# Low halves of weight pieces computed on GpSimd during two kinds of stage, in a two-sequence hybrid encoder

## The chip, the cores and the metric

The kernel runs on 1 core of one Trainium2 chip, as one launch. The metric is device time in microseconds, and lower is better. The engines are named as the profile names them: PE is TensorE (PEld its weight loads), DVE is VectorE, ACT is ScalarE, POOL is GpSimd, SP issues the DMAs. Each engine works through its own instructions in order and waits on semaphores for the others.

## What is computed

Two sequences, a prompt of 512 tokens and a sample of 256, go through the same two layers. Each layer is a SwiGLU, a mixer of three head groups side by side (RG-LRU, RWKV-7 in both directions, attention), and a second SwiGLU:

```python
def layer(x, c, lp, rope):
    mod = (jax.nn.silu(c) @ lp["w_ada"] + lp["b_ada"])[:, None, :]
    sh1, sc1, g1, sh2, sc2, g2, sh3, sc3, g3 = jnp.split(mod, N_MOD, axis=-1)
    h = rmsnorm(x, lp["norm_g"][0]) * (1 + sc1) + sh1
    x = x + 0.5 * g1 * swiglu(h, lp["ffn_w_in"][0], lp["ffn_w_out"][0])
    h = rmsnorm(x, lp["norm_g"][1]) * (1 + sc2) + sh2
    x = x + g2 * mixer(h, lp, rope)          # concat(LRU, RWKV, attention) @ w_mix_out
    h = rmsnorm(x, lp["norm_g"][2]) * (1 + sc3) + sh3
    x = x + 0.5 * g3 * swiglu(h, lp["ffn_w_in"][1], lp["ffn_w_out"][1])
    return x

def step(st, inp):                           # RWKV: 64x64 state of a head, one token
    r_t, w_t, k_t, v_t, kk_t, b_t = inp
    sa = jnp.einsum("bhvk,bhk->bhv", st, -kk_t)
    st = st * w_t[:, :, None, :] + sa[..., None] * b_t[:, :, None, :] + v_t[..., None] * k_t[:, :, None, :]
    y = jnp.einsum("bhvk,bhk->bhv", st, r_t)
    return st, y
```

Width is 1024, the feed-forward width 2816, and all is in fp32.

## The kernel before

**Dense products.** Activations lie transposed (channels on the partitions, tokens along the row), so a product is a sum over tiles of 128 x 128 weights. For accuracy each fp32 operand is split into a high half in the matmul's own format and a low half, and three products stand for one: high x high, high x low, low x high (`mm3`). Weights are streamed from memory in raw tiles `wr` of up to 1024 columns (4 buffers, `weight_raw`, SP) and taken apart piece by piece, 512 or 128 columns each, in `wload`: ACT copies the raw piece into the high half `wh` (L269), then DVE subtracts that from the raw piece to give the low half `wl` (L270). There are 7 buffers of `wh` and 7 of `wl`, shared by both sequences; a buffer comes free when PE has read it for the last time. There are 1368 pieces, 684 for each sequence. One piece is used by 12 matmuls if it has 512 columns of weights (4 tiles x 3 products) and by 3 if it has 128.

**Two sequences against each other.** `layer_thread` runs once for the prompt (`PS`) and once for the sample (`SS_`). While one sequence is in its RWKV stage, which is a long chain of small matmuls with vector work between them, the dense products of the other fill PE. The order of PE's instructions is written out by `Sched`, a planner with threads, priorities and fixed waiting times (`LAT`): the program puts matmuls on PE in exactly that order and PE keeps to it, so a late operand stops PE there. The other engines' instructions are put in order by the framework's own scheduler.

**Fetching ahead.** `wfill` keeps a queue of converted pieces for each sequence: 4 ahead while the other sequence has its flag `mixing` set, otherwise 1 ahead (`LOOK`, `look`). The flag is set when a sequence has put out its mixer's input product (`mix_in`, 19 tiles `mip`) and cleared when it starts its output product (`wopen`). Between the two lie the end of attention and LRU and the RWKV stage, `rwkv_pair` for two pairs of heads in turn.

**A pair of heads.** `rwkv_pair` has, in this order: a preparation (norm of the keys through `kkp` and a reciprocal square root of some ten tiny DVE instructions, L355 to L362; then `AR` and `BK` at L780 to L792, with POOL's share at L747, L781 and L789); the score products `scps`; four levels of a blockwise triangular inverse (`yps`, `dps`); a chain over chunks of 64 tokens (`saps`, `stps`, `zps`, with POOL's `spt` at L970); and an end part, in which the result `ywp` is normalised (L996 to L1006, again with the tiny instructions of a reciprocal square root), transposed through `yp` and multiplied by the gate.

**Stages by the clock of the profile.** The prompt's `mix_in` runs from 486 to 701 us and again from 2025 to 2224; its RWKV stage from 701 to 1020 and from 2224 to 2547, beside the sample's feed-forward (`pb`, `ops`). The sample's `mix_in` runs from 1005 to 1187 and from 2780 to 2899; its RWKV stage from 1187 to 1466 and from 2899 to 3176, beside the prompt's feed-forward (`pg`, `pu`, `ops`).

Of the kernel before, what the change touches and what calls it, by code (L numbers as in the profile page):

```python
# [7 lines left out]
F32 = mybir.dt.float32  # L8
# [3 lines left out]
ALU = mybir.AluOpType  # L12
# [99 lines left out]
def trunk_kernel(ctx, tc, xT, cT, wadh, wada, wfi, wfo, wmi, wmo, prm, gatew, loraw, cst, rope, scanm, outT, dbg=None):  # L112
    nc = tc.nc
    V, A, G, PE = nc.vector, nc.scalar, nc.gpsimd, nc.tensor
# [79 lines left out]
    PS, SS_ = Seq(0), Seq(1)  # L194
# [69 lines left out]
    def wtile(dt, name):  # L264
        return wsp.tile([128, 512], dt, name=name, tag=name)

    def wload(raw, n):
        hi, lo = wtile(F32R, "wh"), wtile(F32R, "wl")
        A.activation(out=hi[:, :n], in_=raw, func=AF.Copy)  # L269
        V.tensor_tensor(out=lo[:, :n], in0=raw, in1=hi[:, :n].bitcast(F32), op=ALU.subtract)  # L270
        return hi, lo

    def weight_units():
        for l in range(DEPTH):
            for fi in range(2):
                if fi == 1:
                    for mt in range(19):
                        yield wmi[l, mt]
                    yield None
                    for m in range(8):  # L280
                        yield wmo[l, m]
                prev = None
                for f0, nf in GROUPS:
                    for p in range(f0, f0 + nf):
                        yield wfi[l, fi, 2 * p]
                        yield wfi[l, fi, 2 * p + 1]
                        if prev is not None:
                            for m in range(8):
                                yield wfo[l, fi, m, :, prev[0] * 128:(prev[0] + prev[1]) * 128]
                            prev = None  # L290
                    prev = (f0, nf)
                for m in range(8):
                    yield wfo[l, fi, m, :, prev[0] * 128:(prev[0] + prev[1]) * 128]

    def weight_raw(u):
        raw = wsp.tile([128, 1024], F32, name="wr", tag="wr", bufs=NR)
        nc.sync.dma_start(out=raw[:, :u.shape[-1]], in_=u)
        return raw

    def weight_list(q):  # L300
        us = weight_units()
        if q is PS:
            raws = [weight_raw(next(us)) for t in range(4)]
            for c in (0, 512):
                for raw in raws:
                    yield raw[:, c:c + 512], 512
        for u in us:
            if u is None:
                yield None
                continue  # L310
            n = u.shape[-1]
            raw = weight_raw(u)
            for c in range(0, n, 512):
                yield raw[:, c:min(c + 512, n)], min(512, n - c)

    def wfill(q, n):
        while len(q.wq) < n:
            if q.wnext is None:
                q.wnext = next(q.wl, False)
                if q.wnext is None:  # L320
                    q.wstop = True
            if q.wnext is False or q.wstop:
                break
            q.wq.append(wload(*q.wnext))
            q.wnext = None

    def wopen(q):
# [701 lines left out]
    def layer_thread(q, th):  # L1029
# [18 lines left out]
        for l in range(DEPTH):  # L1048
# [18 lines left out]
            M = Mix()  # L1067
            M.stage, M.orw, M.lru_done = 0, [], False
            tl = [sch.spawn(attention(q, l, M)), sch.spawn(lru(q, l, M))]
            yield from mix_in(q, l, xs, M)  # L1070
            q.mixing = True
            xs = None
            n2.x = None
            yield lambda: all(t.done for t in tl)
# [51 lines left out]
    with tc.manual_schedule(engines={mybir.EngineType.PE}):  # L1126
        head = Norm(PS, 0, 0)
        for m in range(KD):
            head.add(m, V)
        head.stats()  # L1130
        for q in (PS, SS_):
            q.wl, q.wq, q.wnext, q.wstop, q.mixing = weight_list(q), [], None, False, False
        mods_done.update(((0, 0), (0, 1)))
        first = [(dbank(name="pg"), dbank(name="pu")) for p in range(2)]
        fb = [b for f in first for b in f]
        app = head.apply()
        fw = []

        def head_mm(c):
            for k in (2 * c, 2 * c + 1):  # L1140
                if k % 4 == 0:
                    fw[:] = [wget(PS) for b in fb]
                xh, xl = head.x[k]
                z = (k % 4) * 128
                for b, (wh, wl) in zip(fb, fw):
                    for i, (wt, xt) in enumerate(((wh, xh), (wh, xl), (wl, xh))):
                        mm(b, wt[:, z:z + 128], xt, start=(k == 0 and i == 0), stop=(k == KD - 1 and i == 2))

        for c in range(4):
            ada_head(c)  # L1150
            next(app)
            next(app)
            if c == 0:
                wfill(PS, 4)
            if c > 0:
                head_mm(c - 1)
        head_mm(3)
        th = {}
        th[0] = sch.spawn(layer_thread(PS, th), dense=True, prio=1)
        th[1] = sch.spawn(layer_thread(SS_, th), dense=True, prio=-2)  # L1160
        sch.spawn(ada_rest(), prio=-1)
        sch.run()
# [111 lines left out]
```

## Time and profile before

| | us |
|---|---|
| median of 3 runs | 3485.95 (3485.34 to 3487.81) |
| the profiled execution, its own time | 3480.19 |
| its span, first to last instruction | 3478.4 |
| PE busy in the span | 3344.5 (96%) |
| DVE busy | 2011.8 (58%), 906.0 of it at L270 |
| ACT busy | 1441.6 (41%) |
| POOL busy | 525.2 (15%) |

The busy share of an engine is an average over stages with different limits, so the profile is to be read stage by stage. A busy PE can still be a PE that works through small matmuls at the pace of another engine; what tells is where it sits idle, at which granted clock it runs, and how long before its first use an operand was ready.

### The profile page before, as it was taken

The numbers are of one execution on the slowest core, as the hardware profiler recorded it, in microseconds if no ns is written. First come the engines' busy times: TensorE is split into PE (matmuls) and PEld (weight loads), VectorE is DVE, ScalarE is ACT, GpSimd is POOL, SyncE is SP. The second block draws the span as 40 slices with busy tenths as digits, with TensorE's granted clock in tenths as the row PEclk, the third lists the DMA queues.
The fourth block names the chain that finished last, engine by engine and source line by source line (L and its number), as shares of the span: only waits on it lengthen the run. The fifth ranks groups of instructions, "written<-read, shape, count | busy, mean of one in ns | idle before, by whom it ended". The sixth has DMA issues, their size and how long they took to land.

```text
span 3478.4 us, 69138 instructions
## 1 busy us (share of the span) xinstructions
PE 3344.5 (96%) x28052; PEld 2742.5 (79%) x28052; DVE 2011.8 (58%) x3973; ACT 1441.6 (41%) x2730; POOL 525.2 (15%) x659
## 2 busy tenths in 40 slices
PE   7999999989889999999999999989899999999999
PEld 6777776678877777888888876778789978778899
DVE  4433365776667645556333476657567676456466
ACT  3322244644345533334333337434345564334354
POOL 1100020222121211112000111212211112111010
PEclk9999999999989999999999999999899999999999
DMA  7666674133243222333333331233245533223455
GB/s 279 217 210 199 211 261 142 61 100 115 87 152 97 94 81 78 122 99 122 91 94 91 124 106 57 74 107 103 82 150 170 174 116 101 68 86 119 146 179 161
DMA packets 151629, 445.79 MB, mean 128 GB/s; under 512 B 16912, under 2 KB 20752, under 8 KB 151312
## 3 DMA queue, kind: packets, MB, share of 16 engines
q1 hardware_dynamic: 151312, 441.39, 39.7%
q8 instruction: 220, 3.60, 0.4%
q14 instruction: 97, 0.79, 0.1%
HBM read 427.17 MB, written 14.16 MB: 127 GB/s over the span
## 4 chain that ended last, share of the span: by engine, by line
PE 67%; DVE 7%; issue 3%; ACT 2%; POOL 1%; DMA 0%; POOLq 0%; DVEq 0%; ACTq 0%
PE ops L148 20%; PE pb L148 11%; PE pg L148 11%; PE pu L148 11%; PE mip L148 5%; DVE wl L270 2%; PE dps L148 1%; PE yps L148 1%; DVE nx L411 1%; PE S L148 1%; PE avp L148 1%; PE ywp L148 1%; DVE SC L829 1%; PE ptp L163 1%; ACT wh L269 1%
## 5 line engine op out<-in xcount | busy, mean ns | idle before, releaser
L269 ACT ACTIVATE wh<-wr 128x512 fp32r<-128x512 f32 (+1 forms) x1368 | 812.6, 600 | 1605.3 <-PE ops L148 518.6
L270 DVE TENSOR_TENSOR wl<-wr,wh 128x512 fp32r<-128x512 f32 (+1 forms) x1368 | 906.0, 668 | 783.4 <-ACT wh L269 750.7
L148 PE MATMUL ops<-an,wh 128*128 128x512 f32 (+1 forms) x2816 | 718.2, 346 | 15.5 <-POOL an L351 6.4
L148 PEld LDWEIGHTS ops<-an,wh 128*128 128x128 f32 x2816 | 483.8, 191 | 90.2 <-issue 10.1
L148 PE MATMUL pb<-xn,wh 128*128 128x256 f32 x2816 | 526.9, 288 | 1.0 <-issue 1.0
L148 PE MATMUL ops<-an,wl 128*128 128x512 f32 (+1 forms) x1408 | 479.4, 340 | 5.6 <-DVE wl L270 5.5
L148 PEld LDWEIGHTS pb<-xn,wh 128*128 128x128 f32 x2816 | 438.5, 191 | 18.0 <-issue 10.5
L148 PE MATMUL pg<-xn,wh 128*128 128x512 f32 x1408 | 449.2, 400 | 0.0
L351 POOL TENSOR_TENSOR an<-sg,an 128x512 fp32r<-128x512 f32 (+1 forms) x176 | 201.7, 1146 | 1632.8 <-ACT an L350 1524.3
L148 PE MATMUL pu<-xn,wh 128*128 128x512 f32 x1408 | 448.1, 399 | 0.0
L148 PE MATMUL pb<-xn,wl 128*128 128x256 f32 x1408 | 399.8, 284 | 18.9 <-DVE wl L270 17.0
L430 DVE SCALAR_TENSOR_TENSOR x<-ops,gat,x 128x512 f32<-128x512 f32 (+1 forms) x352 | 215.9, 614 | 215.9 <-PE ops L148 210.7
L148 PE MATMUL mip<-xn,wh 128*128 128x512 f32 (+1 forms) x1216 | 317.4, 351 | 4.2 <-DVE xn L417 1.9
L148 PEld LDWEIGHTS pg<-xn,wh 128*128 128x128 f32 x1408 | 260.5, 189 | 66.1 <-issue 4.3
L148 PEld LDWEIGHTS pu<-xn,wh 128*128 128x128 f32 x1408 | 259.7, 188 | 66.1 <-issue 7.6
L148 PEld LDWEIGHTS ops<-an,wl 128*128 128x128 f32 x1408 | 269.6, 191 | 39.3 <-DVE wl L270 6.1
L148 PEld LDWEIGHTS pb<-xn,wl 128*128 128x128 f32 x1408 | 269.0, 191 | 23.0 <-DVE wl L270 20.1
L148 PE MATMUL pg<-xn,wl 128*128 128x512 f32 x704 | 277.6, 394 | 2.2 <-DVE wl L270 2.2
L148 PE MATMUL pu<-xn,wl 128*128 128x512 f32 x704 | 276.7, 393 | 0.0
L148 PEld LDWEIGHTS mip<-xn,wh 128*128 128x128 f32 x1216 | 211.2, 194 | 45.1 <-issue 11.6
L148 PE MATMUL mip<-xn,wl 128*128 128x512 f32 (+1 forms) x608 | 208.5, 343 | 2.2 <-DVE wl L270 2.2
L148 PEld LDWEIGHTS pg<-xn,wl 128*128 128x128 f32 x704 | 133.0, 189 | 33.7 <-DVE wl L270 2.6
(256 smaller groups left out, 3727.2 us busy)
## 6 DMA issues: line engine op xcount, KB each, us to landing
wr<-in_wfi_dram SPq DMA_DIRECT2D x352, 512.0 KB, 3.6
adaw<-in_wada_dram SPq DMA_DIRECT2D x128, 512.0 KB, 4.4
wr<-in_wfo_dram SPq DMA_DIRECT2D x192, 256.0 KB, 2.7
wr<-in_wfo_dram SPq DMA_DIRECT2D x128, 320.0 KB, 2.9
wr<-in_wmi_dram SPq DMA_DIRECT2D x76, 512.0 KB, 3.6
wr<-in_wmo_dram SPq DMA_DIRECT2D x32, 512.0 KB, 3.5
adaw<-in_wadh_dram SPq DMA_DIRECT2D x32, 256.0 KB, 5.2
xsp<-x SPq DMA_DIRECT2D x8, 512.0 KB, 3.0
```

The costliest lines, as they stand in the source:

```text
L148: PE.matmul(out, lhsT, rhs, start=start, stop=stop, skip_group_check=True)
L163: PE.transpose(out, src, idn)
L269: A.activation(out=hi[:, :n], in_=raw, func=AF.Copy)
L270: V.tensor_tensor(out=lo[:, :n], in0=raw, in1=hi[:, :n].bitcast(F32), op=ALU.subtract)
L351: eng.tensor_tensor(out=lo, in0=src, in1=hi.bitcast(F32), op=ALU.subtract)
L411: V.scalar_tensor_tensor(out=t, in0=q.x[k], scalar=scl[l][:, i, k, q.i:q.i + 1], in1=self.rB, op0=ALU.mult, op1=ALU.mult)
L430: V.scalar_tensor_tensor(out=q.x[m], in0=ps, scalar=gat[l][:, i, m, q.i:q.i + 1], in1=q.x[m], op0=ALU.mult, op1=ALU.add)
L829: V.tensor_tensor(out=SC[h][d][:, c0:c0 + 4, :], in0=pp[h].rearrange("p (c x) -> p c x", x=128), in1=smask[d].unsqueeze(1).to_broadcast([1 ...
```

## The change

The low half is computed by POOL instead of DVE in two cases: while the other sequence has `mixing` set, and while the piece's own sequence is in `mix_in` (new flag `inmix`). In all other cases DVE goes on computing it. The instruction is the same one, a subtraction of two operands in SBUF. Nothing else is edited; PE's instructions and their order stay the same to the last row.

```diff
-    def wload(raw, n):
+    def wload(q, raw, n):
         hi, lo = wtile(F32R, "wh"), wtile(F32R, "wl")
         A.activation(out=hi[:, :n], in_=raw, func=AF.Copy)
-        V.tensor_tensor(out=lo[:, :n], in0=raw, in1=hi[:, :n].bitcast(F32), op=ALU.subtract)
+        eng = G if (SS_ if q is PS else PS).mixing or q.inmix else V
+        eng.tensor_tensor(out=lo[:, :n], in0=raw, in1=hi[:, :n].bitcast(F32), op=ALU.subtract)
         return hi, lo
...
-            q.wq.append(wload(*q.wnext))
+            q.wq.append(wload(q, *q.wnext))
...
+            q.inmix = True
             yield from mix_in(q, l, xs, M)
-            q.mixing = True
+            q.mixing, q.inmix = True, False
```

In the built program 567 of the 1368 low halves stand on POOL, 511 of 512 columns and 56 of 128; POOL has 1226 instructions where it had 659. (Line numbers behind `wload` are higher by one in the changed kernel: L270 becomes L271, L781 becomes L782.)

The first place is the preparation of the prompt's first pair (703 to 736 us in the profile). On POOL, from `csum` to `aa` (`AR` and `aa` are the preparation's own steps, `an` belongs to the sample's feed-forward), there stood before:

```order
L747 TENSOR_SCALAR csum<-csum 128x1024
L753 MEMSET Pt 128x8
L754 MEMSET Pt 128x8
L768 COPY PC<-Pt 128x8
L781 TENSOR_TENSOR AR<-f,Pt 128x512
L769 COPY PC<-Pt 128x8
L351 TENSOR_TENSOR an<-sg,an 128x256
L781 TENSOR_TENSOR AR<-f,Pt 128x512
L789 TENSOR_TENSOR aa<-aa,f 128x1024
```

and now, from the second `AR` on:

```order
L782 TENSOR_TENSOR AR<-f,Pt 128x512
L271 TENSOR_TENSOR wl<-wr,wh 128x512 x6
L790 TENSOR_TENSOR aa<-aa,f 128x1024
L271 TENSOR_TENSOR wl<-wr,wh 128x512 x6
L352 TENSOR_TENSOR an<-sg,an 128x256
```

Six low halves stand between the preparation's last two steps on POOL, and more between the earlier ones. On DVE, in the same place, from the normalised keys on (`x` is the sample's residual), there stood before:

```order
L762 TENSOR_TENSOR kb<-kb,rB 128x512
L430 SCALAR_TENSOR_TENSOR x_112<-ops,gat_134,x_112 128x256
L780 SCALAR_TENSOR_TENSOR AR<-kb,Pt 128x512 x2
L783 SCALAR_TENSOR_TENSOR csum<-aa,kb 128x1024
L270 TENSOR_TENSOR wl<-wr,wh 128x512
L786 SCALAR_TENSOR_TENSOR BK<-csum,cu 128x8x64 x2
L430 SCALAR_TENSOR_TENSOR x_113<-ops,gat_134,x_113 128x256
L270 TENSOR_TENSOR wl<-wr,wh 128x512
L788 TENSOR_SCALAR aa<-aa,kah_3965,ka_0_3963 128x1024
L270 TENSOR_TENSOR wl<-wr,wh 128x512
```

and now:

```order
L763 TENSOR_TENSOR kb<-kb,rB 128x512
L431 SCALAR_TENSOR_TENSOR x_112<-ops,gat_134,x_112 128x256
L781 SCALAR_TENSOR_TENSOR AR<-kb,Pt 128x512 x2
L784 SCALAR_TENSOR_TENSOR csum<-aa,kb 128x1024
L431 SCALAR_TENSOR_TENSOR x_112<-ops,gat_134,x_112 128x256
L787 SCALAR_TENSOR_TENSOR BK<-csum,cu 128x8x64 x2
L431 SCALAR_TENSOR_TENSOR x_113<-ops,gat_134,x_113 128x256
L789 TENSOR_SCALAR aa<-aa,kah_3965,ka_0_3963 128x1024
```

The low halves are gone from between the preparation's steps on DVE; the steps themselves keep their order. The second place is the end part of the same pair (837 to 848 us); on POOL there stood before, between the chain over chunks and the next pair:

```order
L970 TENSOR_SCALAR spt<-S_7809,PC 128x64 x12
L351 TENSOR_TENSOR an<-sg,an 128x256 x3
L1014 TENSOR_TENSOR yy<-yy,kb 128x512
L351 TENSOR_TENSOR an<-sg,an 128x256
L747 TENSOR_SCALAR csum<-csum 128x1024
```

and now, from the last `spt` on:

```order
L971 TENSOR_SCALAR spt<-S_7809,PC 128x64 x2
L271 TENSOR_TENSOR wl<-wr,wh 128x512 x2
L352 TENSOR_TENSOR an<-sg,an 128x256
L271 TENSOR_TENSOR wl<-wr,wh 128x512 x5
L352 TENSOR_TENSOR an<-sg,an 128x256
L271 TENSOR_TENSOR wl<-wr,wh 128x512 x3
L352 TENSOR_TENSOR an<-sg,an 128x256
L271 TENSOR_TENSOR wl<-wr,wh 128x512 x2
L1015 TENSOR_TENSOR yy<-yy,kb 128x512
```

Twelve low halves now stand on POOL ahead of the step `yy` of the end part.

## Rows read from the trace of the kernel before

**Rows 1.** Busy time by stage: length, busy us of each engine, clock, DMA share, GB/s.

```profile
core 0: us, PE busy (x) PEld busy (x) DVE busy (x) ACT busy (x) POOL busy (x), PEclk, DMA share, GB/s
701.00:1020.00 319.00, 284.99 (x4744) 253.85 (x4743) 215.13 (x448) 132.65 (x262) 67.76 (x86) 0.94 0.36 115
...
1187.00:1466.00 279.00, 278.63 (x2662) 217.30 (x2662) 149.16 (x326) 96.17 (x193) 41.74 (x59) 1.00 0.29 88
...
2224.00:2547.00 323.00, 287.11 (x4777) 258.84 (x4776) 211.52 (x441) 134.00 (x263) 74.18 (x89) 0.92 0.34 105
```

**Rows 2.** The same view for the prompt's four preparations and one end part.

```profile
703.00:736.00 33.00, 28.52 (x209) 25.18 (x208) 28.55 (x57) 17.42 (x34) 10.17 (x9) 1.00 0.40 124
853.00:886.00 33.00, 30.27 (x226) 27.58 (x226) 29.01 (x53) 16.72 (x29) 10.96 (x10) 0.96 0.35 108
2226.00:2260.00 34.00, 30.37 (x217) 27.23 (x217) 25.97 (x51) 15.74 (x32) 13.99 (x12) 0.95 0.26 75
2379.00:2412.00 33.00, 29.00 (x204) 26.78 (x201) 26.84 (x50) 15.66 (x27) 11.09 (x10) 0.90 0.38 118
835.00:850.00 15.00, 14.29 (x167) 13.78 (x164) 12.97 (x32) 7.53 (x15) 1.52 (x2) 1.00 0.37 106
```

**Rows 3.** Busy time of the low halves alone on DVE: length, busy us, count.

```profile
703.00:736.00 33.00, 12.96 (x19) 1.00 0.40 124
716.29:733.62 17.33, 7.34 (x11) 1.00 0.59 182
837.18:847.78 10.60, 4.10 (x6) 1.00 0.40 116
```

**Rows 4.** Groups by shape: line, engine, operation, count, busy us, mean ns, idle before.

```profile
L270 DVE TENSOR_TENSOR wl<-wr,wh 128x512 fp32r<-128x512 f32 x1240 | 867.3, 705 | 705.2 <-ACT wh L269 676.4 <-PE ops L148 10.0 <-PE pu L148 5.9
...
L351 POOL TENSOR_TENSOR an<-sg,an 128x512 fp32r<-128x512 f32 x88 | 116.9, 1329 | 1056.9 <-ACT an L350 1056.9
...
L270 DVE TENSOR_TENSOR wl<-wr,wh 128x128 fp32r<-128x128 f32 x128 | 40.6, 317 | 78.2 <-ACT wh L269 74.3 <-PE ops L148 2.0 <-PE saps L148 1.7
```

**Rows 5.** Timeline of PE in the first preparation and end part: start, us, idle before.

```profile
710.83 1.02 PE L148 MATMUL kkp<-ksq,cs 128*128 128x512 f32 x2
...
727.43 0.39 PE L148 MATMUL pb<-xn,wl 128*128 128x256 f32 x1 [2.26 <-DVE wl L270]
...
736.22 0.37 PE L148 MATMUL scps<-AR,BK 64*128 64x128 f32 x1
...
848.62 1.15 PE L148 MATMUL yp<-cs,yy 64*64 64x64 f32 x32 [0.70 <-DVE yy L1006]
```

**Rows 6.** Timeline of DVE in the first preparation.

```profile
716.29 0.70 DVE L367 STREAM_TRANSPOSE tT<-kkp 128x512 f32<-128x512 f32 x1
...
731.21 2.48 DVE L270 TENSOR_TENSOR wl<-wr,wh 128x512 fp32r<-128x512 f32 x1
733.62 1.28 DVE L792 TENSOR_TENSOR BK<-aa,cu 128x512 f32<-128x512 f32 x2
```

**Rows 7.** Timeline of POOL, end of the first preparation and end part.

```profile
730.37 2.77 POOL L789 TENSOR_TENSOR aa<-aa,f 128x1024 f32<-128x1024 f32 x1 [14.75 <-DVE aa L788]
...
842.34 0.76 POOL L351 TENSOR_TENSOR an<-sg,an 128x256 fp32r<-128x256 f32 x1 [12.67 <-PE pb L148]
```

**Rows 8.** Timeline of DVE in the end part of the first pair.

```profile
837.18 0.69 DVE L996 TENSOR_REDUCE st<-ywp 128x8 f32<-128x512 f32 x1 [1.54 <-PE ywp L148]
...
842.40 0.72 DVE L360 TENSOR_TENSOR nt<-y 128x8 f32<-128x8 f32 x1
...
844.58 0.17 DVE L360 TENSOR_TENSOR nt<-y 128x8 f32<-128x8 f32 x1
...
847.78 0.69 DVE L1006 TENSOR_TENSOR yy<-yy,rs 128x512 f32<-128x512 f32 x1
```

**Rows 9.** Waits of PE between 2224 and 2547 us: total us, times, longest.

```profile
PE zps L148 <- DVE S L971: 4.6, 5, 2.5
```

**Rows 10.** Timeline of DVE in the end part of the second pair.

```profile
995.40 0.72 DVE L355 TENSOR_SCALAR sh<-va 128x8 int32<-128x8 int32 x1
```

More of the change, by code (lines that the diff above doesn't have):

```diff
@@ L1131, in trunk_kernel @@
         for q in (PS, SS_):
-            q.wl, q.wq, q.wnext, q.wstop, q.mixing = weight_list(q), [], None, False, False
+            q.wl, q.wq, q.wnext, q.wstop, q.mixing, q.inmix = weight_list(q), [], None, False, False, False
         mods_done.update(((0, 0), (0, 1)))
```

## The prediction, made before the changed kernel was run

> **What bounds the kernel now.** I read the busy time by stage first. PE is busy for 96% of the span, but where it loses time is narrow. In the two RWKV stages of the prompt PE is busy 284.99 of 319 us and 287.11 of 323 us, so it sits idle for 34.0 and 35.9 us, and its granted clock, between the levels of 1.2 and 2.4 GHz, is 0.94 and 0.92 of the upper one on the mean [rows 1]. In the sample's RWKV stage PE is busy 278.63 of 279 us at 1.00 [rows 1]. So the prompt's two stages, in which the sample's feed-forward is to fill PE, are where a change of vector work can move the end; in the sample's a faster DVE gives PE nothing.
>
> Next, what PE waits for there. The prompt's stage holds four pieces of work in which DVE is nearly full: the preparations, where DVE is busy 28.55, 29.01, 25.97 and 26.84 us of 33 or 34, and POOL only 10 to 14 us [rows 2]. Of the first one's 28.55 us, 12.96 are 19 low halves [rows 3]. PE is idle in the four for 4.5, 2.7, 3.6 and 4.0 us, 14.8 together [rows 2]. Two chains meet there. The sample's weights come just in time or late: PE waits 2.26 us for one low half at 727.43 [rows 5]. And the preparation itself is queued on DVE: `kkp` ends at 711.85 on PE, but DVE takes it up at 716.29, 4.4 us later, and puts out the last `BK` at 734.90, 1.3 us ahead of `scps` at 736.22 [rows 5, 6]. The end part is as tight: `yp` starts at 848.62 after a wait of 0.70 us for DVE's `yy` [rows 5]. Whatever lengthens these two chains stops PE, in the order that the planner wrote, nearly one to one.
>
> **What the change removes.** DVE loses 567 low halves. What counts is those in the chains. Between 716.29 and 733.62 the low halves take DVE 7.34 us [rows 3]; the last one, 2.48 us long against a mean of 0.705, sat out POOL's `aa`, for which `BK` has to wait in any case [rows 4, 6, 7], so 1.8 of the 7.34 us would not be won. That leaves 5.5 us, and the earlier start of `kkp`'s reading another 4.4: 9.9 us of preparation chain, if nothing else held it. In the end part six low halves take 4.10 us between 837.18 and 847.78 [rows 3, 8].
>
> **What it adds on POOL.** The nearest row to a 512-column low half on POOL has the same shape and types, another subtraction: 1.329 us, against 0.705 on DVE, 1.89 times as long [rows 4]. For 128 columns I estimate 0.317 x 1.89 = 0.60 us [rows 4]. The 19 low halves of the first preparation fit 13 of 512 and 6 of 128 columns (13 x 0.705 + 6 x 0.317 = 11.1, and 12.96 less the 1.8 of the held one is 11.2) [rows 3, 4]. On POOL they make 13 x 1.33 + 6 x 0.60 = 20.9 us, which with POOL's own 10.17 is 31.1 of 33 us [rows 2]: POOL will be as full as DVE was. In the end part the six low halves make 6 x 1.33 = 8.0 us, with POOL's own 1.52 some 9.5 of 10.6 us, 0.90 of it [rows 2, 3]. Were POOL only slow, the buffers would hide it.
>
> **What it adds on DVE: holds.** DVE and POOL don't run side by side when both read two operands from SBUF. POOL's `aa` runs from 730.37 to 733.14, and the low half that DVE started at 731.21 took 2.48 us and ended at 733.69, its own length after POOL was through [rows 6, 7]. Small steps are held just as long: `nt` of 8 columns takes 0.17 us at 844.58 but 0.72 at 842.40, beside POOL's `an` from 842.34 to 843.10 [rows 7, 8]. The chain steps that read two operands from SBUF are 17 in the preparation (nine tiny ones of the reciprocal square root, `kb`, `AR` twice, `csum`, `BK` four times) and 10 in the end part (nine tiny ones and `yy`). Call h the mean hold of such a step. Below, h is 0 if POOL always happens to be between instructions; above, it is 1.33 x 0.94 = 1.25 us, if each step comes just as POOL has begun its next low half, which is what alternating would give. Arrival at random gives half an instruction times POOL's share, 0.67 x 0.94 = 0.63. I take 0.8: nearer to random, since POOL waits for ACT now and then, but above it, since the tiny steps follow one another and each lets POOL begin the next.
>
> The Trainium skill ("SBUF — State Buffer", section "Who interferes with whom") goes further than these rows. It says that tensor_scalar and copies on VectorE can take both ports too and then block, and are blocked by, GpSimd for a whole instruction. The trace agrees in one place: `sh`, a one-source step, took 0.72 us at 995.40 [rows 10]. By that rule four more steps in each chain would be held, 8 x 4 x 0.8 = 26 us more than my sum.
>
> **The sum.** A preparation changes by 17h - 9.9, less some 0.8 of the 1.3 us of slack before `scps` (ACT has a copy in between): 17h - 10.7. An end part changes by 10h - 4.1 - 1.1, the 1.1 being two steps that are held by 0.55 already (the row at 842.40 is one): 10h - 5.2. There are four of each in the prompt's stages (two pairs, two layers): 108h - 63.6, which at h = 0.8 is +22.8 us. Smaller terms: PE waits 4.6 us for DVE's `S` in the chain over chunks of the second layer [rows 9], which a freer DVE can save, while POOL's `spt` now stands behind two or three low halves; -6 to +8, I take -2. The sample's two norms that fall into the prompt's stages have such two-source steps too: 0 to +8, I take +4. In the sample's RWKV stage (chains of half the columns, no idle PE) and in both `mix_in` I take 0, with +10 as the upper bound. The fetch of weights: PE's 14.8 us of idle time in the preparations go from DVE to POOL as the supplier, 0. Sum +25: the profiled execution's 3480.2 would become 3505. The median of the runs lies 5.8 us above that execution, so the forecast is 3511.
>
> **Rivals.**
> *DVE's relief wins.* If POOL is found between instructions more often, h falls; the sum is zero at h = 0.57. Below h = 0.50 the kernel is faster by 7 us or more. The gain ends where PE has no idle time left to give back: 14.8 us in the preparations [rows 2], 0.7 in each end part [rows 5], 4.6 in the chunks [rows 9], 22 us: 3464, more likely 3472. For it: DVE is plainly the full engine there [rows 2], and PE names DVE's low half [rows 5]. Against it: POOL at 94% is seldom found idle.
> *It cancels.* With h between 0.50 and 0.63, random arrival at the upper edge, the time is 3479 to 3493, say 3486.
> *POOL becomes the bound.* With h near 1.25 the sum is 108 x 1.25 - 63.6 = +71, with `spt` +8: 3565. What speaks for it is 31.1 of 33 us on POOL before any hold by DVE; then PE waits for `wl` from POOL and for `scps` alike. More idle time of PE would also lower the clock, which is 0.94 and 0.92 there now [rows 1]; a fall to 0.90 costs 285 x 0.04 = 11 us more.
> That the change doesn't do what it says is excluded: 567 low halves stand on POOL in the built order.
>
> **Chances.** A measurement of this kernel can tell about 0.2%, 7 us, from no change. Forecast, slower with h from 0.63 to 1: 0.45. POOL as the bound: 0.15. Cancelled: 0.14. DVE's relief wins: 0.26. Slower 0.60, same 0.14, faster 0.26. The range reaches down into the relief's case, to 3468, and up to 3556, short of POOL as the full bound; some 0.1 is left out at either end. As both signs are in it: the forecast's own range is 3494 to 3540.
>
> **What would show it.** Right: in the prompt's four preparations POOL is busy 85% or more and DVE falls below 22 of 33 us, the tiny steps L356 to L363 have a mean well above 0.3 us, `scps` and `yp` stand after a wait, and the preparations last 35 to 40 us. The sample's RWKV stages stay at 277 to 281 us. Wrong: the tiny steps stay at 0.17 to 0.25 us, and the preparations shorten to about 30 us with PE's waits for `wl` gone. What would upset the whole argument is another order of POOL's work in time: if POOL gets its low halves done ahead of the chains, out of the 7 buffers, the holds fall where no chain runs.

## The result: 1.3% slower, and the profile after

The changed kernel takes 3532.2 us (median of 4 runs, 3521.9 to 3534.6) beside 3485.6 for the kernel before: a ratio of 1.0129, 95% interval 1.0107 to 1.0150, so 46.6 us more. The forecast was 3511 us, in a range of 3468 to 3556. The profiled execution took 3532.5 us, 3530.7 of them its span.

The page's busy times and its two groups of low halves (line, engine, operation, count, busy us, mean ns of one) show that the work moved as the change says. Here and below `wl` stands one line lower than in the kernel before.

```profile
PE 3359.6 (95%) x28052; PEld 2754.4 (78%) x28052; DVE 1825.6 (52%) x3406; ACT 1438.1 (41%) x2730; POOL 1200.2 (34%) x1226
...
L271 POOL TENSOR_TENSOR wl<-wr,wh 128x512 fp32r<-128x512 f32 (+1 forms) x567 | 703.3, 1251 | 598.9 <-ACT wh L269 562.0
L271 DVE TENSOR_TENSOR wl<-wr,wh 128x512 fp32r<-128x512 f32 (+1 forms) x801 | 530.3, 668 | 521.3 <-ACT wh L269 500.8
```

The same stretches as in [rows 1], by stage, at the times at which they lie now (columns: length, then busy us of PE, PEld, DVE, ACT and POOL, granted clock, DMA share, GB/s):

```profile
705.00:1041.00 336.00, 290.77 (x4741) 259.70 (x4739) 175.54 (x324) 131.89 (x262) 208.76 (x210) 0.91 0.35 109
1210.00:1492.00 282.00, 279.81 (x2659) 217.99 (x2658) 112.69 (x241) 95.52 (x192) 138.48 (x150) 0.99 0.29 88
2256.00:2591.00 335.00, 286.63 (x4776) 258.91 (x4775) 178.63 (x329) 133.12 (x263) 206.36 (x201) 0.90 0.33 102
```

The prompt's two stages are 17 and 12 us longer, PE is idle for 45.2 and 48.4 us of them (34.0 and 35.9 before), and its clock has fallen by 0.02 to 0.03. DVE is less busy by 40 and 33 us, and that won nothing. And here are the four preparations and the first end part, each cut at the same PE instructions as in [rows 2], to about a microsecond:

```profile
707.00:745.00 38.00, 30.23 (x211) 26.99 (x210) 31.19 (x38) 15.59 (x30) 32.15 (x29) 0.94 0.39 122
868.00:903.00 35.00, 29.76 (x226) 27.17 (x223) 28.07 (x38) 12.53 (x22) 26.42 (x22) 0.97 0.36 112
2258.00:2300.00 42.00, 31.84 (x212) 28.41 (x212) 30.52 (x38) 18.24 (x37) 34.24 (x30) 0.84 0.25 69
2415.00:2454.00 39.00, 28.86 (x204) 26.47 (x202) 28.11 (x37) 13.81 (x25) 30.75 (x27) 0.87 0.36 108
847.00:863.00 16.00, 13.98 (x165) 13.47 (x159) 12.91 (x23) 6.17 (x13) 9.98 (x8) 1.00 0.36 99
```

The preparations take 38, 35, 42 and 39 us in place of 33 or 34. DVE executes 38 instructions in the first where it had 57, and is busy for longer: 31.19 us against 28.55. The time is in the steps themselves. This is DVE's timeline of the first preparation (start, us, engine, line, step), and below it what POOL does at that time:

```profile
719.64 1.16 DVE L358 TENSOR_SCALAR y<-sh 128x16 int32<-128x16 int32 x1
720.84 0.38 DVE L361 TENSOR_TENSOR nt<-y 128x16 f32<-128x16 f32 x1
721.25 1.22 DVE L362 SCALAR_TENSOR_TENSOR nt<-nt,v 128x16 f32<-128x16 f32 x1
722.50 0.39 DVE L363 SCALAR_TENSOR_TENSOR y<-nt,y 128x16 f32<-128x16 f32 x1
722.92 1.21 DVE L361 TENSOR_TENSOR nt<-y 128x16 f32<-128x16 f32 x1
...
731.88 3.07 DVE L781 SCALAR_TENSOR_TENSOR AR<-kb,Pt 128x512 f32<-128x512 f32 x2
```

```profile
719.48 6.72 POOL L271 TENSOR_TENSOR wl<-wr,wh 128x512 fp32r<-128x512 f32 x8 [0.38 <-PE bp L148]
726.14 1.20 POOL L782 TENSOR_TENSOR AR<-f,Pt 128x512 f32<-128x512 f32 x1
727.28 8.82 POOL L271 TENSOR_TENSOR wl<-wr,wh 128x512 fp32r<-128x512 f32 x6
739.97 2.37 POOL L790 TENSOR_TENSOR aa<-aa,f 128x1024 f32<-128x1024 f32 x1 [3.88 <-DVE aa L789]
```

Steps of 0.17 us take 1.2 and 0.38 by turns: the eight low halves of the first POOL line take 1.3 us (512 columns) and 0.46 us (128 columns) by turns, and each DVE step ends just after one of them. Two `AR` take 3.07 us, and 1.28 in the kernel without low halves (an experiment below). Over the whole kernel `nt<-y` of 128x16 went from a mean of 172 to 410 ns; two thirds of these steps belong to other norms and stayed at 0.17, and the nine Newton steps (the tiny steps `nt` and `y`) of the four preparations went from 0.17 to 0.88 us. The last POOL line shows that `aa` did not stand behind low halves: POOL had been idle for 3.88 us when DVE's part of `aa` was done. In the other three preparations it had been idle too, for 6.68, 0.63 and 0.63 us. What this does to PE in the first preparation stands in PE's waits (total us, times, longest), 707 to 766 us:

```profile
PE ops L148 <- DVE x L431: 4.2, 1, 4.2
PE scps L148 <- DVE BK L793: 2.6, 1, 2.6
PE btps L163 <- DVE SC L830: 1.4, 3, 0.8
```

**Where the 46.6 us lie.** PE executes the same 28,052 instructions in all kernels of this study, in the same order but for some neighbouring `scps` and `btps`, so a stretch's growth is the start of its last PE instruction less that of its first, in one trace and in the other. This table adds such differences up against the profiled execution of before (3480.2 us, 5.5 below its median, so the totals come out a few us above the differences of medians). "Preparations" runs from 703 to 755, 853 to 904, 2224 to 2280 and 2379 to 2433 us of the trace of before, up to the levels. In stretches that an experiment leaves alone the difference is up to some 2 us, once 4.7: that much a single stretch can be off.

| us against before | changed | no low half | extra | memsets | y in PSUM |
|---|---|---|---|---|---|
| four preparations | +28.0 | -29.3 | +46.3 | +17.2 | +16.8 |
| four end parts | +6.6 | -1.3 | +20.4 | -0.2 | +4.8 |
| levels and chunks, prompt | -4.9 | -0.2 | +8.7 | +2.1 | -3.4 |
| sample's RWKV stages | +5.5 | +2.1 | +6.1 | +7.1 | +7.0 |
| sample's input part, layer 2 | +9.0 | +0.8 | +15.5 | +0.8 | +9.8 |
| all else | +8.0 | +0.3 | +23.1 | +4.5 | +6.3 |
| total | +52.3 | -27.6 | +120.0 | +31.5 | +41.2 |

### The profile page after: what moved, and what is told of

Its sections match the earlier page's. It is cut to its first block, busy times and chain, and to the rows that moved or that the text cites. A ratio compares the mean times of both kernels' runs of the same rounds, so it can differ in the third digit from the quotient of the medians.

```text
span 3530.7 us, 69152 instructions
## 1 busy us (share of the span) xinstructions
PE 3359.6 (95%) x28052; PEld 2754.4 (78%) x28052; DVE 1825.6 (52%) x3406; ACT 1438.1 (41%) x2730; POOL 1200.2 (34%) x1226
## 4 chain that ended last, share of the span: by engine, by line
PE 62%; DVE 6%; issue 2%; POOL 1%; ACT 1%; DMA 0%; POOLq 0%; ACTq 0%; DVEq 0%
PE ops L148 19%; PE pg L148 10%; PE pu L148 10%; PE pb L148 9%; PE mip L148 5%; PE S L148 1%; PE avp L148 1%; DVE nx L412 1%; PE dps L148 1%; PE yps L148 1%; PE gps L148 1%; PE ptp L163 1%; PE ywp L148 1%; POOL wl L271 0%; DVE xn L418 0%
## 5 line engine op out<-in xcount | busy, mean ns | idle before, releaser
L271 POOL TENSOR_TENSOR wl<-wr,wh 128x512 fp32r<-128x512 f32 (+1 forms) x567 | 703.3, 1251 | 598.9 <-ACT wh L269 562.0
L271 DVE TENSOR_TENSOR wl<-wr,wh 128x512 fp32r<-128x512 f32 (+1 forms) x801 | 530.3, 668 | 521.3 <-ACT wh L269 500.8
L148 PEld LDWEIGHTS pb<-xn,wh 128*128 128x128 f32 x2816 | 437.4, 191 | 21.3 <-issue 13.4
L148 PEld LDWEIGHTS pb<-xn,wl 128*128 128x128 f32 x1408 | 268.4, 191 | 19.6 <-DVE wl L271 10.7
```

The source lines that it names most:

```text
L148: PE.matmul(out, lhsT, rhs, start=start, stop=stop, skip_group_check=True)
L271: eng.tensor_tensor(out=lo[:, :n], in0=raw, in1=hi[:, :n].bitcast(F32), op=ALU.subtract)
```

## Experiments

**Theory:** POOL's low halves read SBUF and hold VectorE's two-source steps; where such steps form the chain that PE waits for (the preparations), the hold costs more than the relief gives. **Rival:** POOL is a slow supplier with a queue in order, and PE or later POOL steps wait for it, wherever the pieces are.

### Which of the moved pieces cost

```
-        eng = G if (SS_ if q is PS else PS).mixing or q.inmix else V
e1 +     eng = G if q is SS_ and PS.mixing else V
e2 +     eng = G if q is PS and SS_.mixing else V
e3 +     eng = G if q.inmix else V
```

> GpSimd takes the low halves only for the sample's weights while the prompt is in its RWKV stage; all others stay on VectorE. Theory (GpSimd holds VectorE's two-source SBUF steps, and only the prompt's four preparations are short of VectorE): most of the loss is here. PE's starts of the whole change were late by 30 us over the four preparations, gained 6 over the chunk parts and were flat in the end parts, so 25 to 32 us above the kernel before, 3511 to 3517 us. Rival (the 46 us come from GpSimd being a slow supplier wherever it stands, in proportion to the pieces moved): these are about 250 of 567 pieces, so 20 us, and then the other two parts carry the rest in proportion.

> GpSimd takes the low halves only for the prompt's weights while the sample is in its RWKV stage. Theory: the sample's steps are half as wide and PE is never out of work there, so a step on VectorE that is held has slack; PE's starts moved by 3.6 and 2.0 us in the first preparation of each layer's stage and by nothing after. Expected 3 to 7 us above the kernel before, 3488 to 3493 us. Rival (loss in proportion to the pieces moved): some 200 of 567 pieces, 16 us, 3502 us.

> GpSimd takes the low halves only for the mixer's input weights of the sequence itself. Theory: 10 to 15 us above the kernel before (3495 to 3501 us), nearly all of it in the sample's input part of layer 2, where PE's starts moved by 9 us, because no other sequence has work to put under it there and the sample's short convolution and norm steps on VectorE and GpSimd are waited for; the prompt's own input parts give 2 to 4. If the cause of those 9 us were the RWKV stage before (lateness carried on), this kernel would show none of them: 3486 to 3490 us.

Measured: e1, with 241 of the 567 pieces, 3512.1 us, 1.0074 (1.0062 to 1.0087) of the kernel before; e2, 181 pieces, 3485.4 us, 1.0003 (0.9994 to 1.0012); e3, 145 pieces, 3498.0 us, 1.0036 (1.0024 to 1.0049). That is 26.6, 0 and 12.6 us: 39 of the 46.6, not in proportion to the pieces. For e2 a loss of 3 to 7 us was expected, and none came. The remaining 7 us appear only with all parts together and stay unexplained; they are about as large as the errors of the three.

e2 is the instructive one. The holds are there: the sample's `BK` steps, 691 ns on the mean before, are as long as in the changed kernel, and the time doesn't move, although the sample's chain is held. In that stage PE had no idle time [rows 1]; that the chain has slack there is inferred from the unmoved time.

```profile
L793 DVE TENSOR_TENSOR BK<-aa,cu 128x256 f32<-128x256 f32 x8 | 9.8, 1265 | 4.4 <-POOL aa L790 4.4
```

e3's loss is where the trace of the changed kernel has +9.0: the sample's input part of layer 2, 9.8 us. There the short convolution `xc` is a chain of twelve two-source and one-source steps on DVE. The kernel before, 2775 to 2870 us, and then e3, 2780 to 2890:

```profile
L555 DVE SCALAR_TENSOR_TENSOR xc<-zp,pr,xc 128x256 f32<-128x256 f32 x9 | 4.3, 483 | 0.4
L553 DVE TENSOR_SCALAR xc<-zp,pr 128x256 f32<-128x256 f32 x3 | 1.2, 408 | 0.0
```

```profile
L556 DVE SCALAR_TENSOR_TENSOR xc<-zp,pr,xc 128x256 f32<-128x256 f32 x9 | 10.6, 1178 | 0.5
L554 DVE TENSOR_SCALAR xc<-zp,pr 128x256 f32<-128x256 f32 x3 | 3.8, 1278 | 0.2 <-ACT zp L548 0.2
```

That is 8.9 us more. ACT then waits for DVE's `y`, which stands right behind `xc` (1.5 us before), and PE's wait in front of `mip` for ACT's `y` rises from 1.2 to 6.0 us:

```profile
ACT y L568 <- DVE y L567: 10.9, 2, 5.7
```

PE keeps to its written order and stops there, although the prompt's `pg` and `pu` also run in that stretch. The second line of each pair is a one-source step, and it is held like the others: 408 ns before, 1278 in e3.

The fourth kernel of this set leaves the pieces of the preparation and of the input part with DVE:

```
-        eng = G if (SS_ if q is PS else PS).mixing or q.inmix else V
+        o = SS_ if q is PS else PS
+        eng = G if o.mixing and not o.prep else V
 (o.prep is set at the start of rwkv_pair and cleared ahead of the levels)
```

> As the changed kernel, but VectorE keeps the low halves from the first step of a sequence's RWKV preparation up to its levels, and for the mixer's input weights; GpSimd has them in the levels, the chunk chain and the end part. Theory: the preparation's loss (30 us) and the input part's (10 to 13) are gone, the chunk chain's gain (6 us over four) stays, the end parts are even, and pieces made ahead at the edges cost up to 3: 3477 to 3488 us, no slower than the kernel before. Rival (the loss is GpSimd's slowness as a supplier of low halves, wherever PE takes them as fast as they come): the levels and chunks take most of the pieces, so 15 us or more stay, 3500 us.

Measured: 3481.9 us, 0.9993 (0.9984 to 1.0002), with 255 pieces on POOL. Pieces in the levels, chunks, end parts and the sample's stage cost nothing, and gain nothing that can be told from no change. The gain in "levels and chunks" of the changed kernel's column isn't shown either: e2 and e3, in which nothing changes in that stage, scatter from -0.8 to +2.6 us there.

### Relief and hold apart

```
e6   hi = wtile(F32R, "wh"); A.activation(out=hi, ...)
   + if (SS_ if q is PS else PS).mixing or q.inmix:
   +     return hi, hi
e7   V.tensor_tensor(out=lo, in0=raw, in1=hi, op=ALU.subtract)
   + if (SS_ if q is PS else PS).mixing or q.inmix:
   +     G.tensor_tensor(out=z, in0=hi, in1=hi, op=ALU.subtract)
e8 +     G.tensor_copy(z[:, 0:1], hi[:, 0:1]); G.memset(z, 0.0); G.memset(z, 0.0)
e9 +     G.tensor_scalar(z, hi, 1.0, None, ALU.add)
 (e8 and e9 stand in place of the last line of e7; column indices are left out)
```

> As the changed kernel, but in the changed places no engine makes the low half: PE reads the high half in its place (the low part of these weights is left out of the result; PE's work is the same in number and size). So VectorE is relieved and GpSimd is not loaded: the relief alone. Theory: the prediction's other term alone, minus 64 us at four preparations and four end parts by its sum, less what another wait then takes over; PE idles 34 and 36 us in the prompt's two stages before, some of it not VectorE's, so minus 25 to minus 64 us, 3422 to 3461 us. Rival (VectorE's low halves were hidden, nothing to gain): 3478 to 3486 us; then the holds of the changed kernel are just its 46 us and no more.

> As the kernel before (VectorE makes all low halves), and GpSimd beside it makes, in the places of the change, an extra subtraction of the same size from two SBUF operands into a tile that nobody reads. The holds alone, with no relief. Theory: relief and holds are separate terms, so this is the kernel before plus 46 us plus the relief that the kernel without low halves shows, 70 to 110 us: 3556 to 3596 us. Rival (the loss was PE waiting for GpSimd's low halves): nobody waits for this result, so only the queue on GpSimd (aa, an, AR, XT behind it) shows, at most 15 us: 3486 to 3501 us.

> As the kernel with the extra subtraction, but in its place a copy of one column of the high half (so that it starts at the same point) and two memsets of the tile, about as long in all (1.2 us by 0.3 us for 256 columns) with nothing read but the column. GpSimd's queue is as full, its reads of SBUF are gone. Theory (the hold comes from GpSimd's reading and writing beside VectorE's two reads): well under a third of the extra subtraction's cost, 3486 to 3510 us. Rival (the loss comes from GpSimd's own later steps behind the pieces in its queue): as much as the extra subtraction, to within its shorter time.

Measured: without low halves 3449.3 us, 0.9889 (0.9875 to 0.9904), that is -37 us; with the extra subtraction 3602.3 us, 1.0329 (1.0316 to 1.0342), +116; with the memsets 3513.8 us, 1.0075 (1.0062 to 1.0088), +27. The first gives the time of a kernel that leaves out work. So the relief is real. POOL's instructions, with DVE still making its low halves, cost three times as much (70 to 110 us were expected), and a POOL that is as full but nearly only writes costs a quarter of that (3513.8 us, where 3510 were expected at most). The mean of `nt<-y` 128x16 (172 ns before) beside the extra subtraction, then beside the memsets:

```profile
L363 DVE TENSOR_TENSOR nt<-y 128x16 f32<-128x16 f32 x36 | 12.2, 339 | 0.7
```

```profile
L365 DVE TENSOR_TENSOR nt<-y 128x16 f32<-128x16 f32 x36 | 6.2, 172 | 0.7
```

The Trainium skill ("SBUF — State Buffer", section "Who interferes with whom") says that a two-input step of VectorE contends with GpSimd instructions that read SBUF and not with those that only write; these two rows agree.

The two terms don't add up to the change. By the table, -27.6 and +120.0 make 92.4, and the change is 52.3: in the preparations the sum is too small (17.0 against 28.0), everywhere else it is too large (75.4 against 24.3). One difference is seen: beside the extra subtractions DVE still makes low halves, and they are held too, 800 ns on the mean at 512 columns in place of 705. What a hold costs in the changed kernel is therefore taken below from its difference to the kernel without low halves, and not from this run.

```profile
L270 DVE TENSOR_TENSOR wl<-wr,wh 128x512 fp32r<-128x512 f32 x1240 | 983.7, 800 | 654.5 <-ACT wh L269 632.8 <-PE pu L148 5.9 <-PE ops L148 4.6
```

Why the relief is 7.3 us in a preparation and no more is seen in the busy time of the first two, first of the kernel before (703 to 755 and 853 to 904), then without low halves:

```profile
703.00:755.00 52.00, 45.72 (x405) 40.48 (x406) 45.28 (x87) 27.43 (x50) 13.23 (x12) 0.97 0.40 126
853.00:904.00 51.00, 47.80 (x468) 43.35 (x470) 44.94 (x83) 26.62 (x46) 14.72 (x13) 0.93 0.34 103
```

```profile
701.00:744.00 43.00, 42.67 (x407) 38.84 (x410) 28.52 (x59) 27.68 (x50) 11.45 (x12) 1.00 0.46 153
844.00:889.00 45.00, 44.78 (x526) 41.16 (x529) 27.78 (x59) 26.62 (x46) 12.48 (x13) 1.00 0.41 124
```

PE is full: 42.67 of 43 us, so there is little idle time left to give back. Over the four, PE's idle time falls from 20.7 to 4.1 us, and its busy time for the same matmuls from 192.4 to 179.0, as the granted clock rises (here from 0.97 and 0.93 to 1.00). In the changed kernel it goes the other way by the same two terms: idle 41.8, busy 199.3, with a clock of 0.88 to 0.91.

What are the memsets' 27 us? DVE's waits show it: `BK` waits for POOL's `aa`, which is queued behind them, 24.5 us in all; in the kernel before it was 8.2.

```profile
DVE BK L797 <- POOL aa L794: 24.5, 7, 8.2
```

The next kernel is that of the memsets with `aa` made on DVE (`G.tensor_tensor(out=at_, ...)` became `V.tensor_tensor`):

> As the kernel with the memsets, but the preparation's product aa, which there stands behind them in GpSimd's queue, is made on VectorE. Theory (what the memsets cost, 27 us, is GpSimd's queue and no hold: BK's wait for aa rose from 2.9 to 20.0 us in the prompt's four preparations): the wait goes and VectorE works 1.3 us longer in each, so 10 to 15 us less than with the memsets, 3499 to 3504 us. Rival (the memsets hold something else, such as the buffer of the high half that their one-column copy reads): 3511 to 3519 us as before, or more by VectorE's 5 us.

Measured: 3504.4 us, 1.0047 (1.0031 to 1.0064), 9.4 us less than the memsets: just short of what was expected. The four preparations fall from +17.2 to +3.7. So in the kernel with memsets the queue is a cost by itself, and `aa` is its place. In the changed kernel, where POOL sat idle in front of `aa`, it is not.

> As the kernel with the extra subtraction, but the extra instruction on GpSimd is a one-source tensor_scalar over the same columns (high half plus one into a tile that nobody reads). It asks whether GpSimd holds VectorE by any read of SBUF or by reading two operands. If any SBUF read holds: the short steps of the preparation stay at 0.30 to 0.35 us and the time lies in proportion to its busy time near the extra subtraction's 3602, above 3560 us. If only two-source instructions hold: the short steps are back at 0.172 us as beside the memsets, and the time is that of GpSimd's queue alone, 3500 to 3520 us. I expect the second, 3514 us.

Measured: 3551.8 us, 1.0185 (1.0165 to 1.0206): neither. The short steps are nearly free, as I expected:

```profile
L363 DVE TENSOR_TENSOR nt<-y 128x16 f32<-128x16 f32 x36 | 7.6, 210 | 0.7
```

But the extra instruction now takes 1738 ns on the mean, where the subtraction took 1332, and `BK` waits 23.7 us for `aa` behind it. Its shortest execution takes 1.48 us and the subtraction's 1.03, so a part of this is its own length. Since the two instructions differ in length, this run doesn't say how much of its 65 us is hold and how much queue, and the question whether one source is enough to hold stays half open.

```profile
L273 POOL TENSOR_SCALAR xtra<-wh 128x512 f32<-128x512 f32 x511 | 888.0, 1738 | 459.5 <-ACT wh L269 440.6 <-ACT SAV L957 2.2 <-PE zps L148 2.0
```

The kernels with extra work also keep the high half's buffer a little longer, and `wh` on ACT waits for that (98 us in all with the one-source instruction); what this costs PE was not separated.

### How long a hold is

> As the changed kernel, but each low half of 512 columns on GpSimd is made by two instructions of 256 columns, about 0.76 us each in place of 1.335, so GpSimd is busy 0.18 us more for each of 511 pieces. Theory (a tiny step of VectorE waits out one GpSimd instruction, 1.2 us by turns with 0.38): shorter instructions halve what each short step waits; the tiny steps of the preparation (13 of them) give back 0.5 us for every second one, 3 to 4 us for each preparation, so 8 to 16 us below the changed kernel, 3516 to 3524 us. Rival (GpSimd's throughput bounds): 85 us more busy on GpSimd makes it slower than the changed kernel, 3535 to 3560 us.

```
e5 + for c in range(0, n, n // 2): eng.tensor_tensor(out=lo[:, c:c + n // 2], ...)   # on GpSimd, n = 512
```

Measured: 3521.2 us, 1.0095 (1.0082 to 1.0108), 11 us below the changed kernel, although POOL is busy for 96 us more. The length of the single instruction matters here and not POOL's throughput: the Newton steps of the four preparations fall from a mean of 0.88 to 0.63 us.

> As the changed kernel, but in the short chain of the preparation (three Newton steps after kkp) the running value y lies in PSUM, in the bank of kkp, and the products are taken in another order so that each of the nine steps reads one operand from PSUM and one from SBUF; VectorE's other steps are as they were. Theory (GpSimd holds a VectorE step only while it reads two SBUF operands; steps with a PSUM operand, such as x and sg, were not held in the trace of the changed kernel): the nine steps fall from a mean of 0.41 us to 0.2 to 0.25, that is some 2 us by the means and up to 7 by the first preparation's timeline (10.2 us from the first to the last, 3.3 without GpSimd), of which the wider steps behind give a part back: 8 to 20 us below the changed kernel, 3512 to 3524 us. Rival (GpSimd slows every VectorE instruction, or the chain only waits in VectorE's queue): no change, 3528 to 3536 us.

```
e10  y = ps[:, 0:n]       # the bank of kkp, in place of an SBUF tile
   - t = y * y;           t = (t * -0.5) * v;  y = (t + 1.5) * y
   + t = (y * -0.5) * v;  t = t * y;           y = (t + 1.5) * y
```

Measured: 3523.7 us, 1.0110 (1.0095 to 1.0125), 8.5 us below the changed kernel, at the small end of what was expected. DVE's timeline of the first preparation:

```profile
716.91 0.17 DVE L358 TENSOR_SCALAR kkp<-sh 128x16 int32<-128x16 int32 x1
717.11 0.17 DVE L361 SCALAR_TENSOR_TENSOR nt<-kkp,v 128x16 f32<-128x16 f32 x1
717.32 0.17 DVE L362 TENSOR_TENSOR nt<-nt,kkp 128x16 f32<-128x16 f32 x1
717.52 0.18 DVE L363 SCALAR_TENSOR_TENSOR kkp<-nt,kkp 128x16 f32<-128x16 f32 x1
...
720.71 1.21 DVE L763 TENSOR_TENSOR kb<-kb,rB 128x512 f32<-128x512 f32 x1
722.12 2.38 DVE L781 SCALAR_TENSOR_TENSOR AR<-kb,Pt 128x512 f32<-128x512 f32 x2 [0.20 <-DVE kb L763]
...
739.35 3.41 DVE L793 TENSOR_TENSOR BK<-aa,cu 128x512 f32<-128x512 f32 x2 [8.08 <-POOL aa L790]
```

With one source in PSUM a short step takes its own 0.17 us again, beside the same low halves on POOL; the first wide step from SBUF behind them, `kb`, takes 1.21 us in place of 0.70. The Trainium skill ("SBUF — State Buffer", section "Who interferes with whom") says that a VectorE step with at most one SBUF input, outside the two-port modes, doesn't contend; these rows agree. From `tT` to `rB` the chain takes 4.3 us, where the changed kernel needs 11.9. But most of the gain is lost at the end of the chain. Over the four preparations the Newton steps take 25.4 us less, the wide two-source steps 10.5 us more, and `BK` waits 7.3 us longer for `aa`, most of it in the first (8.08 us), where `aa` now stands in POOL's queue. From `tT` to the last `BK` 9.0 of 105.0 us are gone. In the changed kernel the held chain came later than POOL's queue; the queue shows only once the chain is faster.

The last kernel puts e1's choice of pieces, halves, `y` in PSUM and `aa` on DVE together:

> What the runs found, put together: GpSimd takes the low halves only for the sample's weights in the prompt's RWKV stage, in instructions of 256 columns; the preparation's y lies in PSUM; aa is made on VectorE. By the four preparations of the changed kernel, 28 us behind: minus 11 for y in PSUM, minus 8 for halves, minus 13 for the queue in front of aa, plus 5 to 10 for aa's own time on VectorE, of which some is the same microsecond twice, so 0 to 8 us behind there, plus some 4 in the end parts: 3482 to 3498 us, 3490 the middle. If the holds that remain (AR, BK, csum, kb, XT on VectorE) were small beside the 29 us of relief that the kernel without low halves showed, it would come under the kernel before, 3465 to 3478 us.

Measured: 3505.2 us, 1.0048 (1.0034 to 1.0062), above what was expected: 27 us below the changed kernel, and still 18 above the kernel before. Beside e1, which moves the same pieces and is 26.6 us above, the three remedies give back only 8.5, and the two intervals touch. No kernel of the study can be told to be faster than the kernel before, except the one that leaves work out. PE's waits in its first preparation, and then one tile's row (count, duration in ns: least, median, most):

```profile
PE btps L163 <- DVE SC L832: 5.7, 2, 5.4
PE pb L148 <- POOL wl L273: 3.1, 4, 2.3
PE ops L148 <- POOL wl L273: 1.4, 3, 0.7
```

```profile
L883 DVE TENSOR_TENSOR XT<-SC,cs x64: 268/346/6601, 744.5 to 3087.2; 32x256 f32<-32x256 f32 x32, 32x128 f32<-32x128 f32 x32
```

From `tT` to the last `BK` the chain now takes 74.2 us over the four, less than the 76.7 of the kernel before, and still the preparations lose 12.1 us. In the first, POOL is late as supplier (4.5 us), and one `XT` step, of at most 0.42 us in the kernel before, took 6.60 us and held `SC` and `btps` behind it.

## Why the prediction was right, step by step

**What bounds the kernel, and where:** right. e1 and e4 bracket it: the pieces of the preparations carry the loss of the prompt's stages, and in the sample's stage the holds cost nothing (e2).

**What the preparation gains:** oversized. The forecast has -10.7 us each, of which 9.9 are the shorter chain on DVE; the kernel without low halves gives -7.3 (29.3 over four). The step that failed is the 9.9: from `kkp` on PE to the last `BK` the chain is shorter by 6.3 us each (98.4 us over the four before, 73.3 without low halves). Of the 5.5 us that the first was to win between `tT` and `BK` it won 2.8, since `BK` then waits 2.1 us for POOL's `aa`. PE gained more than the chain did, because less idle time also meant a higher clock: 13.4 us of busy time over the four, which the text counts for a loss alone. In the changed kernel `kkp` was indeed taken up sooner, 3.5 us after its start in the first preparation and not 5.5.

**What the hold costs:** the mechanism is right, and the size that fits is made up of other parts. Changed kernel less the one without low halves is 57.3 us in the preparations, 14.3 each; the forecast has 17 x 0.8 = 13.6. But the 17 steps took 68.3 us over the four, and 32.4 without low halves: a hold of 0.53 us a step and not 0.8, or 9.0 us a preparation. (In the first, the nine Newton steps take 8.2 us of DVE where 1.6 would do, and the wide steps 5.0 more.) The four one-source steps of each chain add 1.1 us a preparation. These two make 40.2 of the 40.3 us by which the chain from `tT` to the last `BK` is longer, so POOL's queue has no part in it. PE's idle time is 37.7 us longer accordingly; the other 20.3 us are busy time for the same matmuls at a clock of 0.88 to 0.91 in place of 0.96 to 1.00, which the forecast has only in its third rival. That 14.3 came out near 13.6 is luck: with 0.53 in place of 0.8 the forecast's own sum gives -4 us, its rival of cancelling.

**The end parts:** both terms too large. Forecast -5.2 and +8 each; measured -0.3 and +2.0 on the mean. PE waits only 0.70 us for `yy` in the kernel before [rows 5], so there was little more to gain, and the ten two-source steps were held for 0.12 us each (14.9 us over the four against 10.1 without low halves), not 0.8. `yp` does stand after a wait, 2.02 us in the first.

**The one-source steps:** leaving them out of the sum was wrong. Where a low half ran beside them they were held too. `y<-sh` of the four preparations took 1159, 1147, 1219 and 648 ns, 162 to 174 before, and the same step with its result in PSUM 165 to 178 (the first line of that kernel's timeline above). In the first end part, before and after:

```profile
841.32 0.16 DVE L355 TENSOR_SCALAR sh<-va 128x8 int32<-128x8 int32 x1
```

```profile
854.32 1.01 DVE L356 TENSOR_SCALAR sh<-va 128x8 int32<-128x8 int32 x1
```

Over the four preparations (`v`, `sh`, `y`, `aa`) and the four end parts (`sh`, `y`) such steps are 10.9 us longer than in the kernel without low halves. The prediction names the rule of the Trainium skill ("SBUF — State Buffer", section "Who interferes with whom") that tensor_scalar can block and be blocked; these rows agree, with less than half of the 26 us that it worked out.

**What was taken as nothing:** the input parts. 12.6 us by e3, against an upper bound of 10 that also held the sample's stage. The step that failed is that no row of the input part was read: the twelve `xc` steps stand in a chain there.

**Low halves as supply:** right. PE's waits for low halves in the whole trace are 26.9 us before (17.0 `pb`, 5.5 `ops`, 4.4 others) and 26.3 after, 8.2 of them now by POOL.

**The sum:** the forecast's +22.8 for preparations and end parts is +34.6 in the trace, from a relief of 30.6 in place of 63.6 and a loss of 65.2 in place of 86.4, the clock's part included in both. Two terms were too large in opposite directions, so the +25 owes its right side to luck as much as to the mechanism. It is short by 22 us, of which 12 are this and 9 the sample's input part.

**What was to be seen:** POOL is busy 75 to 85% in the four preparations (85% or more expected), they last 38, 35, 42 and 39 us (35 to 40), the tiny steps have means of 379 to 437 ns at 128x16 (above 300), `scps` and `yp` stand after waits, the sample's first RWKV stage takes 282 us (277 to 281). DVE did not fall below 22 us: a held step counts as busy, which the expectation forgot.

## What to carry to other kernels

Moving a step from VectorE to GpSimd where both read SBUF was no relief by itself here: steps of VectorE's chain that read two operands from SBUF, and one-source steps from SBUF to SBUF beside them, waited out GpSimd instructions, 0.53 us a two-source step in the preparations. Where the time did not depend on the held steps, the move cost nothing and gained nothing (e2, e4). Taking one operand from PSUM freed the short steps, but the wide steps behind them were then held longer, and with the chain's own step out of GpSimd's queue the kernel was still slower than before (e12). Size the gain by how much shorter the waiting engine's chain gets and by how much idle time that engine has, together with what the idle time does to its clock; the loss went much further, to 116 us with the extra subtraction. A kernel in which the moved work is left out, and one in which it is doubled, show the sign and the order of the two terms in two runs; here they did not add up to the change.

## What the hardware showed that was not expected

A held step is not sure to go next when one GpSimd instruction ends. In the last kernel one `XT` step, of at most 0.42 us in the kernel before, took 6.60 us. It began under a low half, and eight more of 0.7 us and an `an` ran back to back on POOL before it ended, 0.3 us after the last:

```profile
744.53 6.60 DVE L883 TENSOR_TENSOR XT<-SC,cs 32x256 f32<-32x256 f32 x1
```

```profile
743.27 4.17 POOL L273 TENSOR_TENSOR wl<-wr,wh 128x256 fp32r<-128x256 f32 x6
747.41 0.72 POOL L354 TENSOR_TENSOR an<-sg,an 128x256 fp32r<-128x256 f32 x1
748.09 2.76 POOL L273 TENSOR_TENSOR wl<-wr,wh 128x256 fp32r<-128x256 f32 x4
```

The Trainium skill ("SBUF — State Buffer", section "Who interferes with whom") speaks, for VectorE's two-port modes, of the other engine being blocked for the whole instruction; this row is longer than any instruction that stood beside it. So halving GpSimd's instructions shortened the mean hold of the Newton steps (0.88 to 0.63 us) and did not bound a single one here.

POOL is held in turn: beside `AR` and `csum` in the first preparation three low halves took 1.74 us each, where the three ahead of them took 1.28.

Small gaps cost nearly twice their length: without low halves 16.6 us less idle time of PE in the four preparations came with 13.4 us less busy time for the same matmuls, at a granted clock of 0.91 to 0.97 before and 0.96 to 1.00 without low halves.
